# A small load ahead of the first load in a log-sum-exp kernel

## The chip, the cores and the metric

The kernel runs on one core of a Trainium2 chip. The metric is device time in microseconds (us), the median of the timed runs. The core has engines that run side by side, each with its own queue of instructions: TensorE (PE in the profile), VectorE (DVE), ScalarE (ACT), GpSimd (POOL) and SyncE (SP). SP computes nothing here; it issues the transfers (DMAs) between the chip's main memory (HBM) and the on-chip memory (SBUF, 128 partitions). The transfers themselves are carried out by 16 DMA engines. Semaphores order the engines among each other, and a DMA counts 16 onto its semaphore when all of it has landed.

## The reference

For each of 32 x 512 = 16,384 rows of 1,024 float32 values the kernel computes the logarithm of the sum of the exponentials:

```python
def reference(x: np.ndarray) -> np.ndarray:
    max_x = np.max(x, axis=-1, keepdims=True)
    return (max_x.squeeze(-1) + np.log(np.sum(np.exp(x - max_x), axis=-1))).astype(np.float32)
```

The input is 67.1 MB, the output 65.5 KB.

## The kernel before

**Tiling.** Each partition is given 128 whole rows (`NC`): 112 (`W`) that lie one behind the other in the input (`x_rows`), and 16 more (`B`) from the last eighth of it (`x_rest`). A row of the input is 4 KB. The data go through one buffer in SBUF, `ring`, of 48 rows to a partition (`RING`), in 18 loads whose sizes in rows stand in the list `LOADS`: three of 16, then one more of 16, 13.5, 12.5, 9, 7, 6, and so on down to 0.47. A load of 16 rows moves 65,536 bytes for each partition, 8.39 MB in all.

**Stages.** The loop at L186 runs over `LOADS`. For each load, SP issues the DMA (helper `load`, L134, issue at L139), with a semaphore of its own (`landed[i]`). Ahead of it stands a wait for whoever last read that part of `ring` (L135 to L137); the first three loads fill the empty ring and wait for nobody. ACT waits for the landing (L196) and takes the exponentials in place (L228). The sums over a row then go one of several ways, by the letter in the list: R, one reduction on DVE (L239); F, POOL adds the halves of the rows (L233) and DVE reduces what is left (L171); T, one DVE instruction to a row that adds the halves and sums (L249); Y and Z, the last row in two pieces, summed by ACT itself (L202). The logarithm of the first 112 rows (L268) is stored from `res` while the rest is under way (L276); the logarithms of the last rows (L279, L281) are stored at the end (L285), 64 bytes for each partition.

**Safety path.** The sums are taken without the subtraction of the maximum. DVE and PE gather whether any sum lies outside of the safe range (L146 to L160, L290 to L308); only if one does, the branch at L319 computes everything again with the maximum subtracted. For this input it is not taken.

**Order.** All order is written by hand: every engine's instructions stand in program order, and the class `Counted` (L30) puts waits in. The program begins with some barriers among the engines and memsets of constants (L62 and L407 in the profile). The function `start_early` (L378), which runs when the program is finalized, takes the first load's DMA instruction out of its place in the body and puts it into the first block, ahead of SP's first drain, so that it is issued before these barriers. At the end SP waits for the other engines (`done`), for the first store (`sp.sem`), clears the range of semaphores from `landed[0]` up to `stored` (L367), and waits for the last store (L369).

Of the kernel before, what the change touches and what calls it, by code (L numbers as in the profile page):

```python
# [52 lines left out]
def kernel(  # L53
# [5 lines left out]
    nc = tc.nc  # L59
# [18 lines left out]
    x_rows = x_flat[0 : P * W].rearrange("(p c) d -> p (c d)", p=P)  # L78
# [5 lines left out]
    def source(e0, size):  # L84
        assert e0 >= W * d or e0 + size <= W * d
        return x_rest[:, e0 - W * d : e0 - W * d + size] if e0 >= W * d else x_rows[:, e0 : e0 + size]
# [8 lines left out]
    def sbuf(name, cols, dtype=fp32, rows=P):  # L95
        return nc.alloc_sbuf_tensor(name, [rows, cols], dtype).ap()

    ring = sbuf("ring", RING * d)
    sumexp = sbuf("sumexp", NC)
    res = sbuf("res", NC)  # L100
    clamped = sbuf("clamped", NC)
# [18 lines left out]
    done = nc.alloc_semaphore("done")  # L120
    again = nc.alloc_semaphore("again")
    ready = nc.alloc_semaphore("ready")
    stored = nc.alloc_semaphore("stored")

    nc.scalar.preload_act_table_set("natural_log_exp_and_others")  # L125
# [8 lines left out]
    def load(i, here, done_before, size):  # L134
        for a, b, who, at in users:  # L135
            if a < here + size and b > here:
                sp.wait(who, at)  # L137
        users[:] = [u for u in users if not (u[0] < here + size and u[1] > here)]
        return nc.sync.dma_start(  # L139
            out=ring[:, here : here + size], in_=source(done_before, size)  # L140
        ).then_inc(landed[i], 16)
# [16 lines left out]
    def add_up(c, who, **kw):  # L158
        pe.wait(*who)
        return pe.did(nc.tensor.matmul(count, lhsT=ones, rhs=sumexp[:, c : c + 1], **kw))  # L160
# [3 lines left out]
    def reduce_folded():  # L164

        nonlocal early_sum
        while folded:
            c0, s0, p0, n0 = folded.pop(0)
            halves = ring[:, p0 : p0 + s0 * d].rearrange("p (c d) -> p c d", d=d)[:, :, 0:H]
            dve.wait(pool, n0)  # L170
            at = dve.did(nc.vector.reduce_sum(  # L171
                out=sumexp[:, c0 : c0 + s0], in_=halves, axis=AX.X
            ))
            users.append((p0, p0 + s0 * d, dve, at))
            if c0 < W:
                early_sum = at
# [3 lines left out]
    here = 0  # L180
# [1 line left out]
    done_before = 0  # L182
    summed_by_act = 0
    ln_early = None
    first_load = None
    for i, (size, ops) in enumerate(loads):  # L186
        if here + size > RING * d:
            assert here == p
            p = here = 0
        if any(q < here + size and q + t * d > here for _, t, q, _ in folded):  # L190
            reduce_folded()
        dma = load(i, here, done_before, size)
        first_load = first_load or dma.ins
        end = here + size
        done_before += size
        act.wait(landed[i], 16)  # L196
        for k, (how, s) in enumerate(ops):
            rows = ring[:, p : p + s * d].rearrange("p (c d) -> p c d", d=d)
            if how in "YZ":

                assert c == LAST and (how == "Z" or here == p)
                at = act.did(nc.scalar.activation(  # L202
                    out=last_exp[:, here - p : end - p], in_=ring[:, here:end], func=AF.Exp,
                    accum_out=first_sum if how == "Y" else last_sum,
                ))
                if how == "Z":
                    last_piece = ring[:, here:end]
                here = end
                if how == "Y":
                    nc.vector.addr_align(128, offset=0, max_nops=0)  # L210
                    dve.wait(act, at)
                    first_piece = dve.did(nc.vector.tensor_copy(out=sumexp[:, LAST:NC], in_=first_sum))  # L212
                summed_by_act = at
            elif how == "A":
                assert here == p
                v = ring[:, p : p + d]
                at = act.did(nc.scalar.activation(
                    out=v, in_=v, func=AF.Exp, accum_out=sumexp[:, c : c + 1]
                ))
                here += d  # L220
                users.append((p, p + d, act, at))
                summed_by_act = at
                who = (act, at)
            else:

                upto = end if k + 1 == len(ops) and c + s < LAST else p + s * d
                v = ring[:, here:upto]
                at = act.did(nc.scalar.activation(out=v, in_=v, func=AF.Exp))  # L228
                here = upto
            if how == "F":  # L230
                reduce_folded()
                pool.wait(act, at)
                at = pool.did(nc.gpsimd.tensor_tensor(  # L233
                    out=rows[:, :, 0:H], in0=rows[:, :, 0:H], in1=rows[:, :, H:d], op=ALU.add
                ))
                folded.append((c, s, p, at))
            elif how == "R":
                dve.wait(act, at)
                who = (dve, dve.did(nc.vector.reduce_sum(  # L239
                    out=sumexp[:, c : c + s], in_=rows, axis=AX.X  # L240
                )))
                users.append((p, p + s * d, *who))
            elif how == "T":
                if c >= W:
                    reduce_folded()
                dve.wait(act, at)
                for r in range(s):
                    lo = rows[:, r, 0:H]
                    who = (dve, dve.did(nc.vector.scalar_tensor_tensor(  # L249
                        out=lo, in0=lo, scalar=1.0, in1=rows[:, r, H:d],  # L250
                        op0=ALU.mult, op1=ALU.add, accum_out=sumexp[:, c + r : c + r + 1],
                    )))
                    users.append((p + r * d, p + (r + 1) * d, *who))
                    if c + r >= LATE:
                        add_up(c + r, who, start=False, stop=False)
            if how == "A" and c >= LATE:
                add_up(c, who, start=False, stop=False)
            if how in "RT":
                if c < W:
                    early_sum = dve.n  # L260
                reduce_folded()
            c += s
            p += s * d
            if c == LATE:

                act.wait(dve, early_sum)
                act.wait(act, early_act)
                ln_early = act.did(nc.scalar.activation(  # L268
                    out=res[:, 0:W], in_=sumexp[:, 0:W], func=AF.Ln
                ))  # L270
                check_early()
            if c <= W:
                early_act = summed_by_act
        assert here == end
# [7 lines left out]
        out=res[:, LAST:NC], in_=last_sum, func=AF.Ln, bias=sumexp[:, LAST:NC]  # L282
# [8 lines left out]
        out=clamped[:, LATE:NC], in0=sumexp[:, LATE:NC], scalar=LOW,  # L291
# [10 lines left out]
        out=over[:, 0:half], in0=last_piece[:, 0:half], scalar=CEILING,  # L302
# [16 lines left out]
    with nc.If(all_fine < 1):  # L319
# [5 lines left out]
        for c0 in range(0, NC, RING):  # L325
# [6 lines left out]
            for c1, c2 in ((c0, edge), (edge, c0 + s)):  # L332
                if c1 == c2:
                    continue
                nc.scalar.dma_start(
                    out=ring[:, (c1 - c0) * d : (c2 - c0) * d],
                    in_=source(c1 * d, (c2 - c1) * d),
# [4 lines left out]
                out=neg, in_=v, op=ALU.max, axis=AX.X, negate=True  # L342
# [3 lines left out]
                out=v, in0=v, in1=neg[:, :, None].to_broadcast([P, s, d])  # L346
# [5 lines left out]
                out=sumexp[:, c0 : c0 + s], in_=v, axis=AX.X  # L352
# [11 lines left out]
    nc.scalar.sem_inc(done, 1)  # L364
    nc.sync.wait_ge(done, 2)
    nc.sync.wait_ge(sp.sem, 16)
    nc.sync.sem_clear(range(landed[0].num, stored.num))  # L367
    kind = dict(sync_type="semaphore", id=stored.num, ant_name="stored")
    nc.sync.add_instruction(mybir.InstEventSemaphore(  # L369
# [8 lines left out]
    def start_early(program):  # L378

        blocks = program.main_func.blocks  # L380
        here = next(b for b in blocks if any(i.name == first_load.name for i in b.instructions))
        k = next(k for k, i in enumerate(here.instructions) if i.name == first_load.name)
        assert not here.instructions[k].has_wait()
        first = here.instructions.pop(k)
        top = blocks[0].instructions
        k = next(
            k for k, i in enumerate(top)
            if i.engine == mybir.EngineType.SP and isinstance(i, mybir.InstDrain)
        )
        top.insert(k, first)  # L390

    nc.at_finalize(start_early)


# [28 lines left out]
```

## Time and profile before

| | |
|---|---|
| timed runs | 161.54, 161.56, 161.56 us; median 161.56 |
| span of the profiled execution, first to last instruction | 160.4 us |
| DVE, ACT, POOL busy | 114.3, 114.5, 37.3 us |
| PE busy | 2.2 us |
| bytes moved by the DMA queue of SP | 67.18 MB |
| instructions in the profile | 219 |

The profiled execution is one run of the program, and its own time is given as its span; what the timed runs have beyond it lies ahead of the first instruction or behind the last. Times in the profile count from the first instruction. A name such as `ring<-in_x_dram` reads "written from"; L139 is line 139 of the kernel. SPq is the queue of SP: its rows are the instructions that issue DMAs. In the table by windows each row has the window, its length, the busy time and count of PE, PEld (weight loads), DVE, ACT and POOL, then the granted TensorE clock, the busy share of the 16 DMA engines and the GB/s that began in that window. A row "KB each, us to landing" counts from a DMA's issue to the increment of its semaphore.

### The profile page before, as it was taken

The page shows a single profiled execution, that of the slowest core. Times are in us where ns is not written, and L with a number is a line of the kernel's source. Part 1 is how long each engine was busy: PE and PEld are TensorE (multiplying, and loading weights), DVE is VectorE, ACT ScalarE, POOL GpSimd, SP SyncE. Part 2 cuts the span into 40 slices and gives each one's busy share as a digit, 9 for nine tenths or more (in the row PEclk, how much of TensorE's full clock was granted, in tenths as well). Part 3 has the DMA queues.
Part 4 walks back from the last instruction along what each step waited for, and adds up shares of the span by engine and source line. Part 5 has one row for each costly group of instructions (what it writes and reads, how often), then busy time and mean ns, then how long its engine had stood idle before and what let it go on. Part 6 is the DMA issues. An engine that isn't in the chain of part 4 may idle for free.

```text
span 160.4 us, 219 instructions
## 1 busy us (share of the span) xinstructions
PE 2.2 (1%) x26; PEld 1.1 (1%) x26; DVE 114.3 (71%) x59; ACT 114.5 (71%) x31; POOL 37.3 (23%) x11
## 2 busy tenths in 40 slices
PE   0000000000000000000000000000000000000022
PEld 0000000000000000000000000000000000000011
DVE  0000000009999499994999859959999999999996
ACT  3000059990699708995099949991999989799996
POOL 0000000000000000000000994690004969891000
DMA  7996996996996996996999999999999999999992
GB/s 262 523 523 262 523 523 262 523 507 278 523 490 294 523 490 294 523 490 294 482 441 441 441 425 409 409 409 480 432 395 417 450 416 398 448 411 424 412 413 95
DMA packets 2881, 67.18 MB, mean 419 GB/s; under 512 B 576, under 2 KB 704, under 8 KB 1344
## 3 DMA queue, kind: packets, MB, share of 16 engines
q1 hardware_dynamic: 2880, 67.18, 97.7%
q14 instruction: 1, 0.01, 0.0%
HBM read 67.11 MB, written 0.07 MB: 419 GB/s over the span
## 4 chain that ended last, share of the span: by engine, by line
DMA 52%; ACT 28%; DVE 19%; issue 1%; PE 0%
DMA ring<-in_x_dram 52%; ACT ring L228 27%; DVE sumexp L239 15%; DVE sumexp L171 2%; DVE ring L249 1%; DVE over L301 0%; PE count L306 0%; ACT res L268 0%; DVE clamped L290 0%; DVE fine L308 0%; DVE sumexp L212 0%
## 5 line engine op out<-in xcount | busy, mean ns | idle before, releaser
L228 ACT ACTIVATE ring<-ring 128x16384 f32<-128x16384 f32 (+16 forms) x23 | 111.7, 4908 | 43.0 <-DMA ring<-in_x_dram 43.0
L239 DVE TENSOR_REDUCE sumexp<-ring 128x16 f32<-128x16384 f32 (+4 forms) x9 | 85.6, 9513 | 42.7 <-ACT ring L228 42.7
L233 POOL TENSOR_TENSOR ring<-ring 128x3072 f32<-128x3072 f32 (+3 forms) x7 | 37.1, 5313 | 107.3 <-ACT ring L228 107.3
L171 DVE TENSOR_REDUCE sumexp<-ring 128x6 f32<-128x3072 f32 (+3 forms) x7 | 18.4, 2656 | 0.0
L249 DVE SCALAR_TENSOR_TENSOR ring<-ring 128x512 f32<-128x512 f32 x15 | 9.6, 687 | 0.4 <-ACT ring L228 0.4
L125 ACT ACT_TABLE_LOAD x1 | 1.3, 1283 | 1.4 <-PEq L62 1.4
L156 PE MATMUL count<-far,bad 128*1 128x1 f32 x2 | 0.2, 164 | 153.2 <-DVE clamped L151 153.2
L160 PE MATMUL count<-sumexp,ones 128*1 128x1 f32 x18 | 1.6, 164 | 3.6 <-DVE ring L249 3.6
L249 DVE DVE_READ_ACCUMULATOR ring<-ring 128x1 f32 x15 | 1.2, 82 | 0.0
L202 ACT ACTIVATE last_exp<-ring 128x544 f32<-128x544 f32 (+1 forms) x2 | 1.2, 584 | 0.0
L126 DVE MEMSET ones<- 128x1 f32 x1 | 0.1, 59 | 1.5 <-PEq L62 1.5
L156 PEld LDWEIGHTS count<-far,bad 128*1 128x1 f32 x2 | 0.1, 80 | 153.2 <-DVE clamped L151 153.2
L160 PEld LDWEIGHTS count<-sumexp,ones 128*1 128x1 f32 x18 | 0.8, 80 | 4.5 <-DVE ring L249 4.5
L301 DVE SCALAR_TENSOR_TENSOR over<-ring 128x240 f32<-128x240 f32 x1 | 0.4, 404 | 0.0
L308 DVE TENSOR_SCALAR fine<-count 1x1 int32<-1x1 f32 x1 | 0.1, 147 | 0.3 <-PE count L306 0.3
L151 DVE SCALAR_TENSOR_TENSOR clamped<-clamped,sumexp 128x119 f32<-128x119 f32 x1 | 0.3, 283 | 0.0
L268 ACT ACTIVATE res<-sumexp 128x112 f32<-128x112 f32 x1 | 0.3, 279 | 0.0
L281 ACT ACTIVATE res<-last_sum,sumexp 128x1 f32<-128x1 f32 x1 | 0.3, 261 | 0.0
L202 ACT ACTIVATION_READ_ACCUMULATOR last_exp<-ring 128x1 f32 x2 | 0.3, 126 | 0.0
L146 DVE TENSOR_SCALAR clamped<-sumexp 128x119 f32<-128x119 f32 x1 | 0.2, 221 | 0.0
L279 ACT ACTIVATE res<-sumexp 128x15 f32<-128x15 f32 x1 | 0.2, 209 | 0.0
L290 DVE SCALAR_TENSOR_TENSOR clamped<-sumexp 128x9 f32<-128x9 f32 x1 | 0.2, 169 | 0.0
(17 smaller groups left out, 1.8 us busy)
## 6 DMA issues: line engine op xcount, KB each, us to landing
ring<-in_x_dram SPq DMA_DIRECT2D x1, 6912.0 KB, 23.9
ring<-in_x_dram SPq DMA_DIRECT2D x1, 6400.0 KB, 19.7
ring<-in_x_dram SPq DMA_DIRECT2D x1, 4608.0 KB, 15.9
ring<-in_x_dram SPq DMA_DIRECT2D x1, 3584.0 KB, 24.0
ring<-in_x_dram SPq DMA_DIRECT2D x1, 3072.0 KB, 19.1
ring<-in_x_dram SPq DMA_DIRECT2D x1, 2288.0 KB, 24.1
ring<-in_x_dram SPq DMA_DIRECT2D x1, 1664.0 KB, 20.9
ring<-in_x_dram SPq DMA_DIRECT2D x1, 1264.0 KB, 23.6
```

The source lines that it names most:

```text
L125: nc.scalar.preload_act_table_set("natural_log_exp_and_others")
L151: dve.did(nc.vector.scalar_tensor_tensor(out=clamped[:, 0:LATE], in0=clamped[:, 0:LATE], scalar=0.0, in1=sumexp[:, 0:LATE], op0=ALU.bypass ...
L156: pe.did(nc.tensor.matmul(count, lhsT=bad[:, 0:1], rhs=far, start=True, stop=False))
L160: return pe.did(nc.tensor.matmul(count, lhsT=ones, rhs=sumexp[:, c : c + 1], **kw))
L171: at = dve.did(nc.vector.reduce_sum(out=sumexp[:, c0 : c0 + s0], in_=halves, axis=AX.X))
L202: at = act.did(nc.scalar.activation(out=last_exp[:, here - p : end - p], in_=ring[:, here:end], func=AF.Exp, accum_out=first_sum if how == ...
L228: at = act.did(nc.scalar.activation(out=v, in_=v, func=AF.Exp))
L233: at = pool.did(nc.gpsimd.tensor_tensor(out=rows[:, :, 0:H], in0=rows[:, :, 0:H], in1=rows[:, :, H:d], op=ALU.add))
L239: who = (dve, dve.did(nc.vector.reduce_sum(out=sumexp[:, c : c + s], in_=rows, axis=AX.X)))
L249: who = (dve, dve.did(nc.vector.scalar_tensor_tensor(out=lo, in0=lo, scalar=1.0, in1=rows[:, r, H:d], op0=ALU.mult, op1=ALU.add, accum_out ...
L268: ln_early = act.did(nc.scalar.activation(out=res[:, 0:W], in_=sumexp[:, 0:W], func=AF.Ln))
L301: dve.did(nc.vector.scalar_tensor_tensor(out=over[:, 0:half], in0=last_piece[:, 0:half], scalar=CEILING, in1=last_piece[:, half : 2 * half ...
```

## The change

A DMA is added that reads the first 16 elements (64 bytes) of each partition's part of `x_rows` into a new tile `scrap` that nobody reads. It is issued by SP, with a semaphore of its own, `opened`. `start_early`, which used to move the first load alone, now moves two instructions in this order: the new DMA, then the first load; both stand ahead of SP's first drain. In SP's queue the new DMA is thus the first instruction and the first load the second. At the end SP also waits for `opened`, which lies in the range of semaphores that it clears. Nothing else is different; `scrap` lies behind `ring` in SBUF, so the small tiles behind it move by 64 bytes.

```diff
     ring = sbuf("ring", RING * d)
+    scrap = sbuf("scrap", 16)
     sumexp = sbuf("sumexp", NC)
...
     ready = nc.alloc_semaphore("ready")
+    opened = nc.alloc_semaphore("opened")
     stored = nc.alloc_semaphore("stored")
...
-    first_load = None
+    opening = nc.sync.dma_start(out=scrap, in_=x_rows[:, 0:16]).then_inc(opened, 16)
+    first_load = [opening.ins]
     for i, (size, ops) in enumerate(loads):
...
         dma = load(i, here, done_before, size)
-        first_load = first_load or dma.ins
+        if i == 0:
+            first_load.append(dma.ins)
...
     nc.sync.wait_ge(sp.sem, 16)
+    nc.sync.wait_ge(opened, 16)
     nc.sync.sem_clear(range(landed[0].num, stored.num))
...
     def start_early(program):
 
         blocks = program.main_func.blocks
-        here = next(b for b in blocks if any(i.name == first_load.name for i in b.instructions))
-        k = next(k for k, i in enumerate(here.instructions) if i.name == first_load.name)
-        assert not here.instructions[k].has_wait()
-        first = here.instructions.pop(k)
-        top = blocks[0].instructions
-        k = next(
-            k for k, i in enumerate(top)
-            if i.engine == mybir.EngineType.SP and isinstance(i, mybir.InstDrain)
-        )
-        top.insert(k, first)
+        for load in first_load:
+            here = next(b for b in blocks if any(i.name == load.name for i in b.instructions))
+            k = next(k for k, i in enumerate(here.instructions) if i.name == load.name)
+            assert not here.instructions[k].has_wait()
+            first = here.instructions.pop(k)
+            top = blocks[0].instructions
+            k = next(
+                k for k, i in enumerate(top)
+                if i.engine == mybir.EngineType.SP and isinstance(i, mybir.InstDrain)
+            )
+            top.insert(k, first)
```

## The prediction

> **What bounds the kernel now.** I read the span with its slices first, then the chain of waits, then the timeline of the first 62 us, and last the table by windows around the start of the first load.
>
> ```profile
> span 160.4 us, 219 instructions
> PE 2.2 (1%) x26; PEld 1.1 (1%) x26; DVE 114.3 (71%) x59; ACT 114.5 (71%) x31; POOL 37.3 (23%) x11
> DMA  7996996996996996996999999999999999999992
> HBM read 67.11 MB, written 0.07 MB: 419 GB/s over the span
> ```
>
> No compute engine is over 71% busy, while the transfers run from the second slice to the last but one. The chain of waits says which of the two the end hangs on:
>
> ```profile
> 1.45 39.86 DMA ring<-in_x_dram
> 41.33 13.87 ACT ring L228
> 72.46 23.87 DMA ring<-in_x_dram
> 119.11 19.09 DMA ring<-in_x_dram
> 138.22 12.34 ACT ring L228 x5
> 150.75 6.06 ACT ring L228 x4
> ```
>
> A DMA entry in this chain is time from issue to landing, and most of it is time in the queue behind earlier loads. The first row is the second load, issued at 1.45: what it waits for is the first load, which was issued at 0.00. So the chain begins with the first load's start, though the view does not name it. The last DMA entry lands at 138.20, where ACT stands idle for it, and from there ACT works through the tail.
>
> ```profile
> 0.00 0.39 SPq L139 DMA_DIRECT2D ring<-in_x_dram  x1
> 1.45 1.28 ACT L125 ACT_TABLE_LOAD   x1 [1.45 <-PEq L62]
> 1.45 0.84 SPq L139 DMA_DIRECT2D ring<-in_x_dram  x2
> 1.83 0.46 SPq L139 DMA_DIRECT2D ring<-in_x_dram  x1
> 22.00 13.86 ACT L228 ACTIVATE ring<-ring 128x16384 f32<-128x16384 f32 x1 [19.27 <-DMA ring<-in_x_dram]
> 41.33 13.86 ACT L228 ACTIVATE ring<-ring 128x16384 f32<-128x16384 f32 x1 [5.46 <-DMA ring<-in_x_dram]
> 60.68 13.86 ACT L228 ACTIVATE ring<-ring 128x16384 f32<-128x16384 f32 x1 [5.49 <-DMA ring<-in_x_dram]
> ```
>
> The first three loads are equal (128 rows of 65,536 bytes), and ACT starts on them at 22.00, 41.33 and 60.68: one every 19.33 to 19.35 us, which is 8.39 MB at 434 GB/s. Each time ACT had been waiting. The first load needs the same 19.33 us of streaming, so 22.00 - 19.33 = 2.67 us pass before its stream runs as if at full rate, issue, ramp and landing together. This 2.67 us is the only place in which the change works.
>
> ```profile
> 0.50:1.00 0.50, 0.00 (x0) 0.00 (x0) 0.00 (x0) 0.00 (x0) 0.00 (x0) 1.00 0.00 0
> 1.00:1.50 0.50, 0.00 (x0) 0.00 (x0) 0.00 (x0) 0.05 (x1) 0.00 (x0) 1.00 4.39 1442
> 1.50:2.00 0.50, 0.00 (x0) 0.00 (x0) 0.15 (x4) 0.50 (x1) 0.00 (x0) 1.00 1.35 524
> 1.90:2.10 0.20, 0.00 (x0) 0.00 (x0) 0.00 (x0) 0.20 (x1) 0.00 (x0) 1.00 1.61 655
> 2.10:4.15 2.05, 0.00 (x0) 0.00 (x0) 0.00 (x0) 0.63 (x1) 0.00 (x0) 1.00 0.00 0
> 4.15:4.75 0.60, 0.00 (x0) 0.00 (x0) 0.00 (x0) 0.00 (x0) 0.00 (x0) 1.00 4.03 1748
> 4.00:8.00 4.00, 0.00 (x0) 0.00 (x0) 0.00 (x0) 0.00 (x0) 0.00 (x0) 1.00 1.21 524
> ```
>
> The last two columns are the share of the 16 DMA engines and GB/s, both booked at a packet's start, so a short window shows how many packets began in it and how long these took. In 1.00 to 1.50 it is 1442 x 0.5 = 721 KB, 11 packets of 65.5 KB, with 4.39 x 0.5 x 16 / 11 = 3.19 us each; in 1.50 to 2.00 four packets of 2.70 us; the last two of the sixteen began in 1.90 to 2.10. Nothing begins in 2.10 to 4.15. All sixteen second packets begin in 4.15 to 4.75, and from then on a packet takes 1.21 x 4 x 16 / 32 = 2.42 us. Eight packets to an engine at 2.42 us are 19.36 us, so an engine that finishes its first packet late stays late. What sets every later landing is thus the **end of the slowest first packet, at up to 4.75**; as if all had begun at full rate between 1.73 and 2.33.
>
> **The change, part by part.** One DMA of 128 rows of 64 bytes (8 KB) is added on SP ahead of the first load; both stand ahead of the first barrier. At the end SP waits for it. Nothing is removed.
>
> *The added issue.* SP issues one DMA after another. The first row of SP above takes 0.39 us; the two loads after the barrier begin at 1.45 and 1.83, 0.38 us apart, and the second of such a pair is itself longer, 0.46 against 0.39. So the first load's issue begins about 0.39 to 0.43 later, and ends at about 0.38 + 0.46 = 0.84 to 0.90 in place of 0.39. I take +0.45 us.
>
> *The opener's packets.* Eight of 64 bytes on each engine. The store of the last 16 columns (L285) has just this size:
>
> ```profile
> 158.95 0.34 SPq L285 DMA_DIRECT2D out_dram<-res  x1
> out_dram<-res SPq DMA_DIRECT2D x1, 8.0 KB, 1.4
> 159.00:159.75 0.75, 0.10 (x2) 0.00 (x0) 0.15 (x1) 0.00 (x0) 0.00 (x0) 1.00 0.00 0
> 159.75:159.80 0.05, 0.00 (x0) 0.00 (x0) 0.00 (x0) 0.00 (x0) 0.00 (x0) 1.00 0.02 3
> 159.95:160.00 0.05, 0.00 (x0) 0.00 (x0) 0.00 (x0) 0.00 (x0) 0.00 (x0) 1.00 0.13 9
> 159.75:160.00 0.25, 0.00 (x0) 0.00 (x0) 0.00 (x0) 0.00 (x0) 0.00 (x0) 1.00 0.37 33
> ```
>
> 144 packets (with the increments) begin within 0.25 us and take 0.37 x 0.25 x 16 / 144 = 0.010 us each: under 0.1 us on an engine. They run while the first load's issue is still under way (0.45 us), so I take 0. Without that cover they cost the 0.1 us. That the first load need not wait for the opener's landing follows from 19.33 us between landings against 19.36 us of packets: from one load to the next no gap is paid.
>
> *The ramp.* This is the unknown. From issue to the first packet the store took 0.80 to 0.85 us and its last packet began within 0.25 us of the first; the first load took 1.00 to 1.10, its sixteen first packets were spread over 1.0 us, and eleven of them ran 0.77 us over 2.42. Either that excess belongs to the first use of the queue, and the opener pays it in the load's place, or it belongs to sixteen 64 KB reads that begin from rest, and the load pays it again 0.45 us later. Best bound: the first load begins like the store, at 0.43 + 0.85 with 0.25 of spread, so by 1.53, and its first packets end by 3.95 in place of 4.75: -0.80. Worst bound: the opener spends the whole ramp of 1.0 us, and the load's own ramp follows behind it: +1.1 with the 0.1 of packets. I take **no gain in the ramp**: the store differs from the first load in size, direction and memory side, and an excess that the opener can only begin to pay at the same 1.0 us as the load does now cannot be over much sooner for it.
>
> *Preamble.* SP reaches the barrier 0.45 later, and so do all engines: ACT's table load would end at 3.2 instead of 2.73, and its first use is at 22; the second and third load are issued at about 1.9 and 2.3 and stand in the queue until 21 and 41. Cover of some 19 us; cost 0.
>
> *The wait at the end.* The opener landed some 150 us before.
>
> ```profile
> SPq L367 <- ACTq L364: 0.7, 1, 0.7
> SPq L369 <- SPq L369: 0.3, 1, 0.3
> ```
>
> Ahead of the clearing at L367 SP idles 0.7 us for ACT, and behind it another 0.3 us for the store; one more satisfied wait lies in there. Queued behind it are only the clearing and the last wait. Without that cover it is one instruction of SP, less than the 0.3.
>
> *Does the shift reach the end?* Every later stage is timed by landings or by engines that follow landings: ACT waits for DMA at 22.00, 41.33, 60.68 and again at 138.22, and the loads in between are issued when DVE frees the ring, which moves with the landings. So the whole schedule moves as one piece, either way. Sum: 160.4 + 0.45 = 160.85. The timed runs lie 161.56 - 160.4 = 1.16 us over the span; with the same, **162.0 us** (+0.28%).
>
> **Rivals.** 0.2% is 0.32 us, about what a measurement of this kernel can tell from no change.
>
> 1. *The opener absorbs the ramp, but it ends no sooner.* The slow start is a fixed time after the first packet of all, until about 2.1; then all sixteen first packets of the load begin together, at 2.1 to 2.2, run 2.42 and end at 4.5 to 4.6 instead of 4.15 to 4.75. The slowest engine gains about 0.15 us: 161.4, within 161.25 and 161.75. For it: packets that began at 1.9 to 2.1 show little excess, those of 1.0 to 1.5 much, so that all ended together whenever they began. Against: nothing in the trace shows a second transfer right behind a cold one. [...]
>
> 2. *The opener warms the path early.* 64 bytes are through long before 64 KB, and the load finds a queue that starts as for the store. The bound is -0.80 (160.75); with half to three quarters of it, -0.4 to -0.6, the time is 161.05. For it: the store's 0.25 us of spread against 1.0. Against: the store is no read from HBM, and the opener's own first packet cannot come before 1.0.
>
> 3. *Two ramps in a row.* The opener's rows touch the same 128 places as the load and pay the spread of 1.0 us, and the load pays its own behind it. Price +1.1 at the most, taken as +0.9: 162.5. It decides if the load's first packets begin after 2.1 and still spread over 1 us. Little speaks for it, since after 4.15 no new row costs anything over 2.42.
>
> 4. *It does not do what it says.* In the program the opener stands first and the load second, both ahead of the barrier, so this one gets no chance of its own.
>
> **How the numbers follow.** Forecast (a plain shift of one issue, 161.9 to 162.15) 0.44; rival 1 0.23; rival 2 0.27; rival 3 0.06. Slower by over 0.2% (above 161.88): nearly all of the forecast's case and rival 3, 0.48. Within 0.2%: rival 1 and the edge of the forecast, 0.22. Faster: rival 2 and a little of rival 1, 0.30. The range goes down through most of rival 2, to 160.9, and up past the forecast's own end by the 0.1 us of packets, to 162.2; it leaves out rival 3 and the lower tail of rival 2, about 0.15. As signs are mixed, the forecast's own range 161.9 to 162.15 stands beside it.
>
> **What would show it.** Right: SP's first two issues 0.38 to 0.43 apart, the sixteen second packets beginning in 4.6 to 5.2, ACT's first start at 22.4 to 22.5, and 19.33 us between landings as before. Rival 1: first starts of the load bunched near 2.1 with 2.42 to 2.6 us each, ACT at 21.8 to 21.9. Rival 2: bunched near 1.3 to 1.6, ACT at 21.4 to 21.6. Rival 3: ACT after 22.9. The prediction is wrong altogether if ACT's first start moves and the end does not move with it by the same amount.

## The result and the profile after

The changed kernel takes 162.27 us, the median of five runs (162.22 to 162.57); the kernel before took 161.56 beside it (161.54 to 161.82). The ratio is 1.0044, 95% interval 1.0031 to 1.0056: 0.71 us slower. It was forecast slower, by 0.44, at 162.0 with a range up to 162.2; the time lies above that range. The profiled execution has a span of 161.2 us and is the longest of the five (162.57). In four later groups of runs the kernel before has medians of 161.66 to 161.69 and the changed kernel 162.26 twice, so about 0.1 of the 0.71 lies with the kernel before in this first group; beside the later ones the loss is 0.57 to 0.59.

The head of the page after, to be laid beside that of before:

```profile
span 161.2 us, 220 instructions
PE 2.2 (1%) x26; PEld 1.1 (1%) x26; DVE 114.3 (71%) x59; ACT 114.5 (71%) x31; POOL 37.3 (23%) x11
DMA  7998998998998998997999999999998999999991
```

Every engine works exactly as long as before; one instruction is more. So the time came as waiting. Where it began shows in the timeline of the first 62 us, the issues of SP ahead of the starts of ACT:

```profile
0.00 0.39 SPq L187 DMA_DIRECT2D scrap<-in_x_dram  x1
0.44 0.42 SPq L141 DMA_DIRECT2D ring<-in_x_dram  x1
1.92 1.28 ACT L127 ACT_TABLE_LOAD   x1 [1.92 <-PEq L62]
22.82 13.86 ACT L232 ACTIVATE ring<-ring 128x16384 f32<-128x16384 f32 x1 [19.62 <-DMA ring<-in_x_dram]
42.16 13.86 ACT L232 ACTIVATE ring<-ring 128x16384 f32<-128x16384 f32 x1 [5.49 <-DMA ring<-in_x_dram]
61.52 13.86 ACT L232 ACTIVATE ring<-ring 128x16384 f32<-128x16384 f32 x1 [5.50 <-DMA ring<-in_x_dram]
```

The load is issued 0.44 us later, but ACT's first start is 0.82 later (22.82 against 22.00). The next two follow at the old distance, 19.34 and 19.36 us. The chain of waits carries the shift to the end:

```profile
1.92 40.22 DMA ring<-in_x_dram
42.16 13.87 ACT ring L232
73.30 23.89 DMA ring<-in_x_dram
119.97 19.08 DMA ring<-in_x_dram
139.07 12.35 ACT ring L232 x5
151.60 6.04 ACT ring L232 x4
```

These are the same pieces as before. The first, which begins with the issue of the second load, begins 0.47 us later; from the second on each is 0.83 to 0.86 us later: 42.16 for 41.33, 139.07 for 138.22, 151.60 for 150.75. The span grew by 0.8. Everything was decided before the first load's landing.

The table by windows shows the start itself:

```profile
1.00:1.40 0.40, 0.00 (x0) 0.00 (x0) 0.00 (x0) 0.00 (x0) 0.00 (x0) 1.00 0.23 20
1.00:1.50 0.50, 0.00 (x0) 0.00 (x0) 0.00 (x0) 0.00 (x0) 0.00 (x0) 1.00 1.37 409
1.50:2.00 0.50, 0.00 (x0) 0.00 (x0) 0.01 (x1) 0.08 (x1) 0.00 (x0) 1.00 4.46 1442
2.40:4.00 1.60, 0.00 (x0) 0.00 (x0) 0.00 (x0) 0.81 (x1) 0.00 (x0) 1.00 0.19 82
3.00:3.50 0.50, 0.00 (x0) 0.00 (x0) 0.00 (x0) 0.21 (x1) 0.00 (x0) 1.00 0.30 131
4.60:5.20 0.60, 0.00 (x0) 0.00 (x0) 0.00 (x0) 0.00 (x0) 0.00 (x0) 1.00 3.79 1638
5.50:5.60 0.10, 0.00 (x0) 0.00 (x0) 0.00 (x0) 0.00 (x0) 0.00 (x0) 1.00 1.51 655
```

In 1.00 to 1.40 there are 8 KB, the opener. The load's first packets begin between 1.40 and 1.50, 1.0 to 1.1 us after the load's issue: the same delay that the load had when it was first of all. Eleven begin in 1.50 to 2.00 and take 4.46 x 0.5 x 16 / 11 = 3.24 us, 0.8 over the steady 2.42, as before (3.19). Two more (82 x 1.6 = 131 KB) begin only after 2.4, one of them after 3.0. Fifteen engines begin their second packet in 4.60 to 5.20, and the last one in 5.50 to 5.60, where before all sixteen lay in 4.15 to 4.75. That last engine sets the landing: its first packet began after 3.0, took 2.4 us (0.30 x 0.5 x 16) and ended at 5.50 to 5.60. The other late one was through with the rest.

### The profile page after: what moved, and what is told of

Read it like the earlier page. It is cut to its first block, busy times and chain, and to the rows that moved or that the text cites. A ratio compares the mean times of both kernels' runs of the same rounds, so it can differ in the third digit from the quotient of the medians.

```text
span 161.2 us, 220 instructions
## 1 busy us (share of the span) xinstructions
PE 2.2 (1%) x26; PEld 1.1 (1%) x26; DVE 114.3 (71%) x59; ACT 114.5 (71%) x31; POOL 37.3 (23%) x11
## 4 chain that ended last, share of the span: by engine, by line
DMA 52%; ACT 27%; DVE 18%; issue 1%; PE 0%
DMA ring<-in_x_dram 52%; ACT ring L232 27%; DVE sumexp L243 15%; DVE sumexp L173 2%; DVE ring L253 1%; DVE over L305 0%; PE count L310 0%; ACT res L272 0%; DVE clamped L294 0%; DVE fine L312 0%; DVE sumexp L216 0%
```

## The experiments

Two theories stood after this. **A**: the load starts one issue of SP later and nothing else; the rest of the 0.7 us is chance in when the last engine begins. **B**: the opener's packets cost more than its issue. Each run was timed beside the kernel before on the same chip; its median was 161.66 to 161.69 in these groups, with single runs of 161.52 to 162.06.

The code below shows the lines that carry each change; what follows from them (the size of `scrap`, the counts that are waited for) is left out.

**Where it stands.** The opener unchanged, then issued by ACT, then by SP behind the load, then replaced by a plain delay (six semaphore increments on SP).

```diff
# on_act
-    opening = nc.sync.dma_start(...)
+    opening = nc.scalar.dma_start(...)
...
-                if i.engine == mybir.EngineType.SP and isinstance(i, mybir.InstDrain)
+                if i.engine == first.engine and isinstance(i, mybir.InstDrain)
# behind
-            first_load.append(dma.ins)
+            first_load.insert(0, dma.ins)
# delay
-    opening = nc.sync.dma_start(...)
-    first_load = [opening.ins]
+    first_load = [nc.sync.sem_inc(opened, 1).ins for _ in range(6)]
...
-    nc.sync.wait_ge(opened, 16)
+    nc.sync.wait_ge(opened, 6)
```

> The changed kernel once more. Theory A (late issue: the load starts one DMA issue, 0.44 us, later, and what is beyond that is chance in when the last of the sixteen engines begins): the time is 162.2 to 162.4 again, but in this profile the last first packet of the load does not have to begin at 3.15; the sixteen second packets begin by 5.2 or so. Theory B (the opener's packets hold up single engines): again one or two engines begin their first packet after 2.4, and ACT starts at 22.6 or later.

> The opener is issued by ACT, ahead of ACT's first drain, so that SP's first instruction is the first load again. Theory A: the issue no longer stands in front of the load; 161.5 to 161.7, ACT's first start at 21.9 to 22.1. Theory B: the opener's packets still share the 16 engines with the load's first packets; 161.8 to 162.0. A warming that helps would show as under 161.4.

> The same two DMAs in SP's queue, the first load first and the opener second. Theory A: 161.5 to 161.65, because only what stands ahead of the load counts. Theory B: the same, since the opener's packets come behind the load's in each engine. If a part of the cost comes with the mere number of instructions or semaphores in the program (the time outside of the span grew by some 0.16 us), 161.7.

> No opener; six semaphore increments on SP stand ahead of the first load instead, so that it is issued late without any other transfer. Theory A: the time grows by the delay that the trace shows for the load's issue (some 0.4 us, 161.95), with the load's packets spread as in the kernel before. Theory B: the same here, so that what the changed kernel has beyond this run's cost per 0.1 us of delay is the opener's packets.

Measured: again 162.26, ratio 1.0035 (1.0021 to 1.0048); on_act 161.71, 1.0005 (0.9996 to 1.0015); behind 161.73, 0.9999 (0.9990 to 1.0008); delay 162.00, 1.0021 (1.0012 to 1.0030). With the load first in SP's queue the opener costs nothing that these runs can tell from zero (0.04 us over the kernel before on ACT's queue, 0.06 behind the load), and it warms nothing either. The timeline of the run with the opener on ACT:

```profile
0.00 0.39 SPq L141 DMA_DIRECT2D ring<-in_x_dram  x1
0.12 0.38 ACTq L187 DMA_DIRECT2D scrap<-in_x_dram  x1
21.83 13.86 ACT L232 ACTIVATE ring<-ring 128x16384 f32<-128x16384 f32 x1 [18.97 <-DMA ring<-in_x_dram]
```

A delay without any transfer costs about what it delays: the load's issue came at 0.38, the time grew by 0.33. That settles that most of the loss is the place in the queue. The supposed growth of the time outside of the span, named in the expectation for "behind", was none of the change: in these groups the kernel before has 1.3 us outside of its span too.

**Issue against packets.** The delay drawn out to the opener's 0.44 us; two openers; an opener for one partition; an opener from rows that the first load does not read.

```diff
# delay7
+    first_load = [nc.sync.sem_inc(opened, 1).ins for _ in range(7)]
# two
-    opening = nc.sync.dma_start(out=scrap, in_=x_rows[:, 0:16]).then_inc(opened, 16)
+    opening = nc.sync.dma_start(out=scrap[:, 0:16], in_=x_rows[:, 0:16]).then_inc(opened, 16)
+    second = nc.sync.dma_start(out=scrap[:, 16:32], in_=x_rows[:, 0:16]).then_inc(opened, 16)
+    first_load = [opening.ins, second.ins]
# one_row
-    opening = nc.sync.dma_start(out=scrap, in_=x_rows[:, 0:16])
+    opening = nc.sync.dma_start(out=scrap[0:1, :], in_=x_rows[0:1, 0:16])
# other_rows
+    opening = nc.sync.dma_start(out=scrap, in_=x_rest[:, 0:16])
```

> Seven semaphore increments in place of six and no opener: the first load is issued at about 0.44, as late as in the changed kernel. Theory A (issue alone): the same time as the changed kernel, ratio 1.0035. Theory B (the issue is 0.4 of it, and some 0.2 more comes from a DMA that stands ahead in the rings): 162.05 to 162.1 on the scale of 161.67 before, ratio 1.0024 to 1.0027.

> Two openers into two parts of the scrap tile, one behind the other, ahead of the first load. Theory A: the load's issue comes at about 0.88 to 0.92, so 162.5 to 162.6. Theory B with an extra for each opener: 162.8 to 162.9; with an extra that comes once, however many there are: 162.7.

> The opener reads 64 bytes for one partition alone, so that one DMA engine has a packet of it and fifteen have none; its issue takes SP as long or nearly so. Theory A: the cost follows the load's issue time (0.35 to 0.45 later, 162.0 to 162.1). Theory B: what is beyond the issue comes from the opener's packets or increments on the sixteen engines; it goes with them, and the time is 162.0 to 162.1 as well, while the last of the first packets begins within 2.1 to 2.3. If it stays at 162.25, a DMA in front costs it whatever its packets.

> The opener reads its 64 bytes from the last eighth of the input, which the first load does not touch. If the opener and the load get in each other's way at the same places in memory, the extra 0.2 goes: 162.05. Theory B without regard to the place: 162.2 to 162.3, with one or two engines beginning their first packet after 2.4.

Measured: delay7 162.12, 1.0026 (1.0017 to 1.0036); two 162.72, 1.0062 (1.0049 to 1.0076); one_row 162.04, 1.0020 (1.0010 to 1.0029); other_rows 162.31, 1.0045 (1.0031 to 1.0059). The plain delay stays 0.15 us short of the opener, and the opener for one partition is cheaper still. Reading from other rows made no difference (162.31 against 162.26). The run with seven increments, its load's issue, ACT's first start and the first packets:

```profile
0.44 0.39 SPq L141 DMA_DIRECT2D ring<-in_x_dram  x1
22.43 13.86 ACT L231 ACTIVATE ring<-ring 128x16384 f32<-128x16384 f32 x1 [19.26 <-DMA ring<-in_x_dram]
```

```profile
1.40:1.90 0.50, 0.00 (x0) 0.00 (x0) 0.00 (x0) 0.01 (x1) 0.00 (x0) 1.00 6.46 2097
2.40:4.00 1.60, 0.00 (x0) 0.00 (x0) 0.00 (x0) 0.77 (x1) 0.00 (x0) 1.00 0.00 0
```

All sixteen first packets (2097 x 0.5 = 1,049 KB) begin in 1.40 to 1.90, and none after 2.4; ACT starts 21.99 us after the load's issue, as before. Two openers move the issue to 0.90 and cost 1.03, so an extra of 0.13 beyond the two issues: once, not for each.

**Which packets.** Sixteen partitions in place of 128 (one packet to an engine, by the count of rows over sixteen engines); 512 bytes for each partition. And two attempts to gain something: the first load itself in two pieces, one row and then fifteen, and in two halves of 64 partitions from SP and ACT; both start from the kernel before.

```diff
# sixteen
+    opening = nc.sync.dma_start(out=scrap[0:16, :], in_=x_rows[0:16, 0:16])
# wide
+    opening = nc.sync.dma_start(out=scrap, in_=x_rows[:, 0:128])
# split, for i == 0
+            for e0, e1 in [(0, 1), (1, 16)]:
+                piece = nc.sync.dma_start(
+                    out=ring[:, e0 * d : e1 * d], in_=source(e0 * d, (e1 - e0) * d)
+                ).then_inc(landed[0], 16)
# halves, for i == 0
+            for who, p0, p1 in [("sync", 0, 64), ("scalar", 64, 128)]:
+                piece = getattr(nc, who).dma_start(
+                    out=ring[p0:p1, 0:size], in_=source(0, size)[p0:p1]
+                ).then_inc(landed[0], 16)
```

> The opener reads 64 bytes for sixteen partitions: one packet and one increment for each DMA engine in place of eight and one. The issue costs the 0.4 us that it cost with one partition. If what is beyond the issue (0.15 to 0.25 us, two engines whose first packet begins after 2.4) hangs on the number of small packets, it is gone or nearly so: 162.05. If any packet or the increment on an engine is enough, 162.2 to 162.3 and again two late engines.

> The opener reads 512 bytes for each partition in place of 64 (the increments and the number of packets are the same). If the extra comes from pieces that are very short, it is gone: 162.05 to 162.1. If it comes from the number of packets and increments, it stays: 162.2 to 162.3. Its bytes alone are 65.5 KB, 0.15 us of the stream if none of it is hidden, so 162.4 bounds it.

> From the kernel before: the first load in two DMAs, one row and then fifteen, both ahead of the barrier, so that the DMA ahead does useful work and the second issue (0.44) is over before the first packets end. If the excess of the first packets (0.7 us each) belongs to 64 KB packets that begin from rest, small packets in front shorten it: 161.2 to 161.5, faster than the kernel before. If it is a fixed time from rest that any load pays once: 161.65. If each DMA in front costs late engines even when it carries the load's own data: 161.9.

> From the kernel before: the first load in two halves of 64 partitions each, one issued by SP and one by ACT, each as the first instruction of its queue. Each engine gets four packets from each. If the time from issue to the end of the first packets is made by one queue handing out the load, two queues shorten it: 161.2 to 161.5. If it is the engines' or the memory's own start, 161.65 to 161.75.

Measured: sixteen 162.12, 1.0030 (1.0018 to 1.0041); wide 162.15, 1.0038 (1.0024 to 1.0053); split 161.58, 0.9998 (0.9989 to 1.0007); halves 181.79, 1.1245 (1.1229 to 1.1261).

The split load is the cleanest test of a warming: here a DMA with packets of 4 KB stands ahead and carries data that are needed. Two issues (0.86 us in all), the first packets running meanwhile:

```profile
0.00 0.86 SPq L195 DMA_DIRECT2D ring<-in_x_dram  x2
21.87 13.86 ACT L235 ACTIVATE ring<-ring 128x16384 f32<-128x16384 f32 x1 [18.67 <-DMA ring<-in_x_dram]
```

```profile
1.00:1.40 0.40, 0.00 (x0) 0.00 (x0) 0.00 (x0) 0.00 (x0) 0.00 (x0) 1.00 0.84 133
```

53 KB begin by 1.4, and ACT starts on the whole load at 21.87, as with the load in one DMA and first in its queue (21.83 to 22.00). Nothing was lost behind this DMA, which does useful work, and nothing was gained from small packets first (161.58 beside 161.66). The slow start has only moved: a packet of 4 KB there takes 0.41 us (0.84 x 0.4 x 16 / 13), where a sixteenth of 2.42 us is 0.15, and the first packets of 60 KB behind them already run at the steady pace:

```profile
3.23:3.45 0.22, 0.00 (x0) 0.00 (x0) 0.00 (x0) 0.00 (x0) 0.00 (x0) 1.00 1.94 838
```

These are three packets (838 x 0.22 = 184 KB) of 1.94 x 0.22 x 16 / 3 = 2.28 us, and 15/16 of 2.42 us is 2.27. That fits the expectation's fixed time from rest that a load pays once (161.65), with first packets of 4 KB as with those of 64 KB. The opener of 8 KB did not pay it in the load's place: most first packets behind it took 3.24 us.

The halves lost 20 us, which none of the expected cases had. In its table by windows:

```profile
4.00:8.00 4.00, 0.00 (x0) 0.00 (x0) 0.00 (x0) 0.00 (x0) 0.00 (x0) 1.00 1.22 262
```

262 GB/s in place of 524 in this window, with the engines as busy: 1.22 x 4 x 16 / 16 packets = 4.9 us for 64 KB. ACT first starts at 42 us. The view of the queues (q1 is SP's, q10 ACT's) shows that the two halves take turns, first in the window from 1 to 3 us, then in that from 5.5 to 7.5:

```profile
q1 hardware_dynamic: 16, 1.05, 243.9%
q10 hardware_dynamic: 16, 1.05, 243.0%
```

Sixteen packets of one half run, then sixteen of the other, so that in these rounds mostly the 64 partitions of one half alone are written. Why a packet then takes 4.9 us in place of 2.42 is not shown by any run here.

**Is the rest real, and is it the short pieces?** The changed kernel and the plain delay on one chip, 256 bytes for each partition, and eight pieces of 64 bytes for each.

```diff
# w256
+    opening = nc.sync.dma_start(out=scrap, in_=x_rows[:, 0:64])
# pieces
+    opening = nc.sync.dma_start(
+        out=scrap.rearrange("p (a b) -> p a b", b=16),
+        in_=x_rows[:, 0:256].rearrange("p (a b) -> p a b", b=32)[:, :, 0:16])
```

> The changed kernel beside the plain delay on the same chip. If the extra beyond the issue is real: 0.15 to 0.25 us above the run with seven increments, and two first packets that begin after 2.4. If it was chance between chips: within 0.05 of it.

> Seven increments and no opener, as before: 0.40 to 0.45 above the kernel before (ratio 1.0025 to 1.0028), and no first packet that begins after 2.4.

> The opener reads 256 bytes for each partition, between the 64 of the changed kernel and the 512 of the earlier run. If the late engines come with pieces under 512 bytes: as the changed kernel, 0.6 over before. If they come with the very short ones alone: 0.45 to 0.5 over before and no first packet after 2.4.

> The opener reads eight pieces of 64 bytes for each partition (512 bytes in all, in 64 packets for each engine instead of 8). If each short piece costs, the extra grows with their number beyond the 0.45 us that the issue hides: 64 x 0.010 = 0.64 us for an engine, so 0.8 to 1.0 over before. If the extra comes once for a DMA with short pieces: 0.6 to 0.65. If short pieces cost nothing: 0.45 to 0.5, as the 512 bytes in one piece.

Measured: after3 162.26, 1.0040 (1.0026 to 1.0054); delay7b 162.08, 1.0028 (1.0017 to 1.0038); w256 162.24, 1.0036 (1.0022 to 1.0050); pieces 162.68, 1.0054 (1.0041 to 1.0068). The opener again lies 0.18 above the plain delay, but the intervals of the two overlap. Its profile, taken on the fastest of its five runs (162.08), has no late engines:

```profile
22.34 13.86 ACT L232 ACTIVATE ring<-ring 128x16384 f32<-128x16384 f32 x1 [19.13 <-DMA ring<-in_x_dram]
```

```profile
1.40:2.40 1.00, 0.00 (x0) 0.00 (x0) 0.15 (x4) 0.48 (x1) 0.00 (x0) 1.00 3.19 1049
2.40:4.00 1.60, 0.00 (x0) 0.00 (x0) 0.00 (x0) 0.81 (x1) 0.00 (x0) 1.00 0.00 0
```

All sixteen began before 2.4, and the time was that of the plain delay. So late engines are not there in every execution. With many pieces there are two again, and ACT starts late:

```profile
0.49 0.57 SPq L141 DMA_DIRECT2D ring<-in_x_dram  x1
22.94 13.86 ACT L232 ACTIVATE ring<-ring 128x16384 f32<-128x16384 f32 x1 [19.54 <-DMA ring<-in_x_dram]
2.75:2.95 0.20, 0.00 (x0) 0.00 (x0) 0.00 (x0) 0.20 (x1) 0.00 (x0) 1.00 1.55 655
5.65:5.75 0.10, 0.00 (x0) 0.00 (x0) 0.00 (x0) 0.00 (x0) 0.00 (x0) 1.00 3.02 1311
```

**Does the late start set the landing?** In the kernel before, the last first packet begins in 1.97 to 2.10 (share 1.31, 504 GB/s there) and takes 1.31 x 0.13 x 16 = 2.72 us, so it ends in 4.69 to 4.82; the last two second packets begin in 4.66 to 4.75 (1456 x 0.09 = 131 KB). I take it from this that an engine's second packet begins where its first ends, so the last second packet marks the end of the slowest first one. In the run with many pieces the two late packets (655 x 0.2 = 131 KB) take 1.55 x 0.2 x 16 / 2 = 2.48 us and are through by 5.43, but two second packets begin only in 5.65 to 5.75, on engines that had begun earlier. The repeat of the changed kernel (`again`) shows the same, and the plain delay of six increments shows one slow engine with no opener at all:

```profile
2.50:2.60 0.10, 0.00 (x0) 0.00 (x0) 0.00 (x0) 0.10 (x1) 0.00 (x0) 1.00 1.57 655
2.70:2.80 0.10, 0.00 (x0) 0.00 (x0) 0.00 (x0) 0.10 (x1) 0.00 (x0) 1.00 1.52 655
5.30:5.40 0.10, 0.00 (x0) 0.00 (x0) 0.00 (x0) 0.00 (x0) 0.00 (x0) 1.00 1.55 655
```

```profile
2.40:4.00 1.60, 0.00 (x0) 0.00 (x0) 0.00 (x0) 0.71 (x1) 0.00 (x0) 1.00 0.00 0
5.20:5.40 0.20, 0.00 (x0) 0.00 (x0) 0.00 (x0) 0.00 (x0) 0.00 (x0) 1.00 0.75 328
```

In the repeat the two late packets take 2.51 and 2.43 us and end by 5.23; the last second packet begins after 5.30, on an engine whose first packet had begun with the others by 2.1 and so took at least 3.2 us. In the run from other rows it is close: the late ones end by 5.26, and the last second packets begin in 5.26 to 5.30. So of these four profiles with packets that begin after 2.4, only the first one of the changed kernel has its landing set by one of them. Nor is 2.4 a sharp line: in the kernel before, whose load is issued at 0.00, two first packets begin in 1.90 to 2.10, and for a load issued at 0.44 that would be 2.34 to 2.54. What does hold is the end of the slowest first packet. In all sixteen profiles in which the first load is one DMA, ACT's first start follows it by 17.2 to 17.3 us, whatever stands ahead.

The profiled executions and the medians side by side (us; the first number is the load's issue, the last is over the kernel before in the same group). The issue and ACT's start are of one execution each, and these scatter: that of `delay` is the slowest of its eleven runs (162.36), that of `after3` the fastest of its five.

| kernel | load issued | ACT's first start, less the issue | packets of the opener per engine | median | over before |
|---|---|---|---|---|---|
| before | 0.00 | 22.00 | none | 161.56 | |
| on_act, behind | 0.00 | 21.83, 21.83 | 8, beside or behind | 161.71, 161.73 | 0.04, 0.06 |
| delay | 0.38 | 22.21 | none | 162.00 | 0.33 |
| delay7, delay7b | 0.44 | 21.99, 21.81 | none | 162.12, 162.08 | 0.43, 0.39 |
| one_row | 0.40 | 21.88 | one on a single engine | 162.04 | 0.35 |
| sixteen | 0.45 | 21.87 | 1 | 162.12 | 0.46 |
| wide, w256 | 0.44, 0.43 | 21.86, 22.14 | 8 of 512 and 256 bytes | 162.15, 162.24 | 0.49, 0.55 |
| after, again, after3 | 0.44, 0.43, 0.44 | 22.38, 22.23, 21.90 | 8 of 64 bytes | 162.27, 162.26, 162.26 | 0.71, 0.59, 0.57 |
| other_rows | 0.44 | 22.10 | 8 of 64 bytes | 162.31 | 0.62 |
| two | 0.90 | 22.44 | 16 of 64 bytes | 162.72 | 1.03 |
| pieces | 0.49 | 22.45 | 64 of 64 bytes | 162.68 | 0.99 |

What follows: of the fifteen runs of the changed kernel in three groups the median is 162.26 and twelve lie above 162.2; of the eighteen with seven increments the median is 162.10 and three do. About 0.43 of the 0.57 to 0.71 us is the later issue. The other 0.15 to 0.3 shows in the medians of the openers with eight packets of 64 bytes on every engine, and is 0.5 with sixty-four (0.99 less the 0.49 of its issue; by the ratio 1.0054, 0.4). At most 0.03 of it is the load's own issue, which takes 0.42 us behind an opener and 0.39 behind the increments. With one packet and one increment to an engine (`sixteen`) the rest is not seen. With eight packets of 512 or 256 bytes the medians leave 0.05 to 0.1, but the ratios, 1.0038 and 1.0036, are those of the changed kernel, so these two decide nothing. Theory A is short by 0.15 to 0.3. Theory B holds for the total; that single engines begin late and so cause it is not shown.

## Why the prediction was right or wrong

**The bound: right.** Nothing but the first load's landing moved, and all later pieces of the chain of waits moved with it by 0.82 to 0.86. The span is 138.4 to 138.5 us longer than ACT's first start in the kernel before and in every experiment but two (`one_row` 138.7, `halves` 138.1). The end of the slowest first packet, which the prediction named as what sets every landing, did set it in each profile. The 1.16 us that the sum adds to the span is no cost: in the experiments each run lies 1.27 to 1.42 over its own span, so the execution that was profiled before (160.4) was probably slower than the median with which the sum paired it. The forecast is that median plus 0.45 all the same.

**The added issue: right.** It was taken as 0.45 from SP's pairs of issues. The load's issue moved by 0.44, and the plain delays, which leave out the transfer, cost 0.33 and 0.39 to 0.43 for 0.38 and 0.44.

**The ramp: right that there is no gain.** Rival 1 (first starts bunched near 2.1, packets of 2.42 to 2.6) and rival 2 (bunched at 1.3 to 1.6, ACT at 21.4 to 21.6) fail on the same rows: the first packets begin 1.0 to 1.1 us after the load's own issue with the opener and without it, and eleven of them take 3.2 us each either way. My evidence for a warming, the store's narrow spread, said nothing about the load: with seven increments the sixteen first packets also began close together, within 0.5 us, and the landing came no sooner (ACT's first start 21.99 us after the load's issue, 22.00 in the kernel before). From the end of its own issue (0.44 + 0.42 = 0.86) the load's first packet came after 0.54 to 0.64 us, in the kernel before after 0.61 to 0.71 (1.00 to 1.10 less 0.39), so about the same.

**The opener's packets: the term that was mis-sized.** It was set to 0, because 0.1 us of packets would run while the load's issue was under way, and 0.1 at the most without that cover. It measured 0.15 to 0.3: the changed kernel lies that far over the kernel before beyond the 0.44 of the issue, and 0.18 over the plain delay on the same chip. The cover argument counted how long the packets occupy an engine, 0.010 us each, and that is indeed short: in the profile they are through by 1.4, before the load's first packet. They do not run while the load is being issued, though, which ends at 0.86 when none of them has begun. What the argument missed is that free engines on the whole are not enough: the landing hung on the slowest of the sixteen (ACT's first start 17.2 to 17.3 us behind the end of its first packet), and a mean over the engines hides it. In the profile of the changed kernel that one began only after 3.0; in its repeat it had begun with the others and took at least 3.2 us. What the opener does to it stays open. The range's upper end, the forecast plus 0.1, had no room for this term, nor for the scatter of a kernel without any opener: the runs with seven increments alone go from 161.99 to 162.48. There is chance in the size of the miss, too. About 0.1 of the 0.71 is the kernel before in the first group, and the forecast was built on its 161.56. Rival 3, the case for more loss, had priced a whole second ramp and was given 0.06; a part of such a loss was the case to name.

**The cover of preamble and end: right.** ACT's table load begins at 1.92 and ends 19 us before its use. At the end SP waits for ACT and for the store as long as it did before, with the added wait in place:

```profile
SPq L372 <- ACTq L368: 0.7, 1, 0.7
SPq L374 <- SPq L374: 0.3, 1, 0.3
```

**What stays open.** Why the slowest first packet ends later behind an opener on all engines was not settled. The size of the pieces is a candidate: the medians fall as the piece grows (0.57 to 0.71, 0.55, 0.49 us over the kernel before for 64, 256, 512 bytes), but the ratios do not (1.0035 to 1.0044, 1.0036, 1.0038), and their intervals overlap, so this is not shown. Nor is it known which engines are the slow ones, since the views of the trace do not name them.

## What to carry to other kernels

Where a stream of transfers sets the end, the first useful DMA should be the first instruction of its queue: whatever was issued ahead of it here was paid in full, at 0.4 us an issue (0.33 us over the kernel before for a plain delay of 0.38, 0.57 to 0.71 for the opener), and a small transfer in front did not make the next one start any faster (1.0 to 1.1 us from issue to first packet, with it and without). Behind the first load or on another queue such a transfer cost nothing that could be measured (0.06 and 0.04 us), but it landed only with the load, 21.5 and 21.9 us after its issue. If something must come first, let it be a piece of the load itself, over all partitions: that took 161.58 here beside 161.66, two halves of the partitions 181.79. When pricing a transfer over sixteen engines, ask for the slowest engine and not for the mean, and give the range the spread that the last of sixteen has.

## What was not expected of the hardware

An opener of 8 KB did not take over the slow start of the load behind it: it was still 1.0 to 1.1 us to the first packet and 3.2 us for most of the first 64 KB packets, which later take 2.42, even when the first 64 bytes of the same rows were read in the half microsecond before. A useful piece of 4 KB to a row did take it over (three packets of 60 KB behind it took 2.28 us each), and nothing was won by it (161.58 beside 161.66). An 8 KB load on ACT's queue, issued 0.12 us behind an 8.4 MB load on SP's, landed only with that load, 21.9 us after its issue:

```profile
scrap<-in_x_dram ACTq DMA_DIRECT2D x1, 8.0 KB, 21.9
q1 hardware_dynamic: 16, 1.05, 241.8%
q10 hardware_dynamic: 16, 0.00, 1.0%
```

The last two lines are the queues in the window from 4 to 5 us: sixteen packets of 64 KB of the load, and beside them sixteen of the opener, as many as there are engines. At that rate, an estimate from this one window, its eight packets to an engine (128 over sixteen) take eight rounds of 2.42 us, as long as the load.

Two DMAs of 64 partitions each, from two queues, moved the first load at half the rate of one DMA of 128 (262 GB/s for 524 between 4 and 8 us), with the halves taking turns in the two windows shown above.
